# A two-layer decoder trunk on one core: rows of x loaded once under a pinned first half-step, and six output columns side by side in the memory attention

## The chip, the cores and the metric

The kernel runs on one core of a Trainium2 chip. A core has a matrix engine (TensorE, PE in the rows, with PEld for its weight loads), a vector engine (VectorE, DVE), a scalar engine (ScalarE, ACT), GpSimd (POOL) and a queue engine (SyncE, SP) that here issues most DMAs. Each takes its own instructions in the order of its program and waits on semaphores for the others. The metric is the device time of one execution in microseconds; lower is better.

## The reference

Two decoder layers act on x, 256 tokens of 1024 features, with a memory of 256 tokens. All weights are float32 and each is used once.

```
for l in range(DEPTH):
    x = x + 0.5 * swiglu(rmsnorm(x, ffn1_norm[l]), ffn1_w_gate[l], ffn1_w_up[l], ffn1_w_down[l])
    h = rmsnorm(x, mix_norm[l])
    x = x + (even_mixer(h, ...) if l % 2 == 0 else odd_mixer(h, ...))
    x = x + memory_cross_attention(rmsnorm(x, xa_norm[l]), mem_n, xa_w_q[l], xa_w_kv[l], xa_w_o[l])
    x = x + 0.5 * swiglu(rmsnorm(x, ffn2_norm[l]), ffn2_w_gate[l], ffn2_w_up[l], ffn2_w_down[l])
return rmsnorm(x, final_norm)
```

`swiglu` is `(silu(x @ w_gate) * (x @ w_up)) @ w_down` with 2816 hidden features. `memory_cross_attention` has 4 heads of 128 features: queries from x, keys and values from the memory, a softmax, and an output projection `o @ w_o` from 512 to 1024 features.

## The kernel before, in words

**Layout.** x stays in SBUF with features on the partitions, as 8 tiles of 128 features by 256 tokens (`x[:, k]`). Weights are a stream of 128x128 tiles in the order of their use: `Stream.take` returns the next. They come from HBM in chunks of 16 tiles (1 MB, four `raw` buffers); blocks of 8 tiles are split into a high part (`whi`, ACT, line 127) and a low part (`wlo`, DVE, line 128: raw minus high), with five buffers of each. A product is done as high by high and low, plus low by high. In the feed-forward step (`mm`, lines 391 and 392) that is one matmul of 512 columns with `whi` and one of 256 with `wlo`; elsewhere (`mm_narrow`, lines 396 to 398) it is three of 256 columns.

**The first half-step** (`ffn1` of layer 0). `w0` holds, for each of the 8 feature tiles, a row of x and four gate-weight tiles side by side (384 KB); `load_first` loads all eight, and later x itself is loaded once more from `xT` in one copy of 1 MB. `gates` runs four gate columns (f = 0 to 3) side by side as the rows land, in two `acc` and two `sc` banks of PSUM. After it `gate_up` does one column at a time: 16 matmuls on one `acc` bank, then `join` (ACT copies one half, DVE adds the other). The sum of squares of x (`squares`) and its mean (`norm_scale`: a small matmul in `sums`, a power on POOL, a transposing matmul in `spread`, an ACT copy into `rbc`) run beside the matmuls. Until `rbc` is there, finished columns wait in `n.waiting`; then `evac` multiplies the gate by `rbc` (DVE), takes the Silu (ACT), multiplies by the up column (DVE) and splits the result into `h` (high part ACT, low part DVE).

**What sets the order.** The builder, `Order`, keeps a clock of PE's work: fillers (the matmul groups) are written out in turn, and tasks put in with `pe.after(delay, fn, cost)` fall in between. That gives a program order, which the framework's scheduler then rearranges for each engine by its own estimates, save for instructions that are marked with `tc.keep_in_program_order`. In `memory` the weight splits are so marked (`ws.pin`).

**The memory attention.** Each of the 4 heads goes through scores, softmax, a turn (`go_turn`, transposing matmuls, line 708, then a split of the probabilities on ACT and DVE, lines 710 and 711) and a weighing with the values (`go_weigh`, lines 725 to 729), whose result is split into `h` (lines 459 and 460). `out_proj` multiplies these four `h` tiles by `w_o`. Columns 0 to 3 stand side by side in four `acc` banks and are fed in parts (heads 0 and 1, then head 2, then head 3); columns 4 to 7 follow one after the other with all four heads. A finished column is added to x (`add_to_x`, DVE, line 454), and the normed tile for the next half-step is made from it (ACT line 316, DVE line 317).

## Time and profile before

| | |
|---|---|
| three timed runs | 970.76, 971.33, 971.44 us; median 971.33 |
| profiled execution | 971.57 us, of which the span of the core's instructions is 969.8 |
| PE busy | 959.2 us, 99% of the span |
| DVE, ACT, POOL busy | 760.2, 614.1, 55.7 us |
| granted TensorE clock | 0.999 of full speed over the span |
| HBM read | 193.51 MB |

The profiled execution lies 0.24 us above the median of the timed ones. Busy time of a matmul in the profile includes the overlap with its neighbours, so PE's 99% is no statement that it runs at its peak; stretches in which fewer matmuls start tell more.

### The profile page before, as it was taken

How to read it: one execution, taken by the hardware profiler on the slowest of the kernel's cores; microseconds unless marked ns; L12 is line 12 of the kernel's file. 1: busy time of each engine (PE TensorE's matmuls, PEld its weight loads, DVE VectorE, ACT ScalarE, POOL GpSimd, SP SyncE). 2: the span in 40 equal slices, each digit the busy share in tenths (PEclk: the TensorE clock that was granted, in tenths of full speed). 3: DMA queues.
4: the chain of work that ended last, by engine and by line, in shares of the span. 5: the costliest groups of instructions: out<-in, count | busy, mean ns of one | idle time of the engine just before them, and what ended most of it. 6: DMA issues, size and time to landing. Idle time of an engine off the chain costs nothing.

```text
span 969.8 us, 16906 instructions
## 1 busy us (share of the span) xinstructions
PE 959.2 (99%) x6536; PEld 899.6 (93%) x6536; DVE 760.2 (78%) x1361; ACT 614.1 (63%) x1144; POOL 55.7 (6%) x95
## 2 busy tenths in 40 slices
PE   9999999999999999999999999999999999999997
PEld 8899999999999999999999999999999999999896
DVE  7988867898878888876778878677878789887663
ACT  7767655697657766665556666556785667666541
POOL 0410000001000000000000000000000003400011
PEclk9999999999999999999999999999999999999999
DMA  9797556555536656556555565565645346775631
GB/s 372 272 333 284 187 205 211 170 189 196 190 111 211 231 191 215 194 198 215 184 208 198 193 218 184 207 208 183 223 147 189 116 167 242 243 253 187 212 131 44
DMA packets 29921, 196.73 MB, mean 203 GB/s; under 512 B 3848, under 2 KB 4872, under 8 KB 7184
## 3 DMA queue, kind: packets, MB, share of 16 engines
q1 hardware_dynamic: 27072, 187.44, 55.5%
q0 software_dynamic: 2192, 7.37, 2.2%
q8 instruction: 51, 0.84, 0.3%
q10 hardware_dynamic: 576, 0.83, 0.2%
q14 instruction: 30, 0.25, 0.1%
HBM read 193.51 MB, written 5.27 MB: 205 GB/s over the span
## 4 chain that ended last, share of the span: by engine, by line
PE 97%; DVE 1%; DMA 1%; ACT 0%; issue 0%; SPq 0%; POOLq 0%; DVEq 0%; ACTq 0%
PE acc L391 41%; PE acc L392 21%; PE acc L397 7%; PE acc L398 7%; PE acc L396 7%; PE acc L574 1%; PE acc L573 1%; PE acc L572 1%; PE acc L918 1%; PE acc L916 1%; PE acc L917 1%; DMA raw<-in_w 1%; PE sc L572 0%; PE sc L574 0%; PE sc L573 0%; DVE wlo L128 0%
## 5 line engine op out<-in xcount | busy, mean ns | idle before, releaser
L127 ACT ACTIVATE whi<-raw 128x1024 fp32r<-128x1024 f32 (+2 forms) x377 | 369.2, 986 | 274.0 <-PE acc L391 133.3
L128 DVE TENSOR_TENSOR wlo<-raw,whi 128x1024 fp32r<-128x1024 f32 (+2 forms) x377 | 426.6, 1136 | 144.7 <-ACT whi L127 141.6
L391 PE MATMUL acc<-x,whi 128*128 128x512 f32 x1392 | 457.4, 383 | 0.9 <-DVE w L402 0.5
L392 PE MATMUL acc<-x,wlo 128*128 128x256 f32 x1392 | 377.4, 273 | 0.6 <-DVE wlo L128 0.6
L391 PEld LDWEIGHTS acc<-x,whi 128*128 128x128 f32 x1392 | 262.2, 189 | 37.4 <-ACT whi L127 1.1
L392 PEld LDWEIGHTS acc<-x,wlo 128*128 128x128 f32 x1392 | 267.2, 192 | 1.9 <-DVE wlo L128 0.9
L391 PE MATMUL acc<-h,whi 128*128 128x512 f32 x462 | 151.3, 382 | 0.0
L392 PE MATMUL acc<-h,wlo 128*128 128x256 f32 x462 | 125.4, 273 | 0.0
L391 PEld LDWEIGHTS acc<-h,whi 128*128 128x128 f32 x462 | 87.1, 189 | 12.0
L392 PEld LDWEIGHTS acc<-h,wlo 128*128 128x128 f32 x462 | 88.7, 192 | 0.2
L396 PE MATMUL acc<-h,whi 128*128 128x256 f32 x322 | 87.2, 279 | 1.6 <-ACT h L459 1.6
L397 PE MATMUL acc<-h,whi 128*128 128x256 f32 x322 | 88.1, 276 | 0.3 <-DVE h L460 0.3
L398 PE MATMUL acc<-h,wlo 128*128 128x256 f32 x322 | 87.8, 275 | 0.0
L402 DVE TENSOR_TENSOR w<-acc,w 128x256 f32<-128x256 f32 x195 | 81.1, 416 | 3.8 <-ACT w L401 3.5
L398 PE MATMUL acc<-x,wlo 128*128 128x256 f32 x304 | 83.9, 278 | 0.0
L397 PE MATMUL acc<-x,whi 128*128 128x256 f32 x304 | 83.8, 277 | 0.0
L396 PE MATMUL acc<-x,whi 128*128 128x256 f32 x304 | 83.4, 279 | 0.0
L401 ACT ACTIVATE w<-acc 128x256 f32<-128x256 f32 x195 | 71.9, 369 | 10.0 <-PE acc L392 9.8
L396 PEld LDWEIGHTS acc<-h,whi 128*128 128x128 f32 x322 | 60.5, 192 | 2.6 <-ACT h L459 2.0
L397 PEld LDWEIGHTS acc<-h,whi 128*128 128x128 f32 x322 | 61.7, 192 | 0.8 <-DVE h L460 0.7
L398 PEld LDWEIGHTS acc<-h,wlo 128*128 128x128 f32 x322 | 61.7, 192 | 0.1
L397 PEld LDWEIGHTS acc<-x,whi 128*128 128x128 f32 x304 | 58.2, 192 | 0.2
(211 smaller groups left out, 1180.7 us busy)
## 6 DMA issues: line engine op xcount, KB each, us to landing
raw<-in_w SPq DMA_DIRECT2D x171, 1024.0 KB, 5.0
dists<-line POOLq DMA_DIRECT2D x2, 1536.0 KB, 13.3
raw<-in_memT SPq DMA_DIRECT2D x3, 1024.0 KB, 5.1
raw<-in_w SPq DMA_DIRECT2D x6, 384.0 KB, 6.8
bias<-dists POOLq DMA_DIRECT2D x2, 1024.0 KB, 11.3
x<-in_xT SPq DMA_DIRECT2D x1, 1024.0 KB, 7.6
tok<-q POOLq DMA_DIRECT2D x32, 32.0 KB, 3.5
bias<-tok POOLq DMA_DIRECT2D x1, 1024.0 KB, 7.7
```

The lines of the kernel that those rows point to most:

```text
L127: for ins in (self.nc.scalar.activation(hi[:, at], src, AF.Copy), self.nc.vector.tensor_tensor(lo[:, at], src, hi[:, at].bitcast(F32), op= ...
L128: self.nc.vector.tensor_tensor(lo[:, at], src, hi[:, at].bitcast(F32), op=ALU.subtract)):
L391: nc.tensor.matmul(ps, w[0], x2.both, start=start, stop=False)
L392: nc.tensor.matmul(ps[:, :S], w[1], x2.high, start=False, stop=stop)
L396: nc.tensor.matmul(ps[:, :S], w[0], x2.high, start=start, stop=False)
L397: nc.tensor.matmul(ps[:, :S], w[0], x2.low, start=False, stop=False)
L398: nc.tensor.matmul(ps[:, :S], w[1], x2.high, start=False, stop=stop)
L401: nc.scalar.activation(halves(out), unpaired(ps[:, S:]), AF.Copy)
L402: nc.vector.tensor_tensor(halves(out), unpaired(ps[:, :S]), halves(out), op=ALU.add)
L572: nc.tensor.matmul(ps, hh, wh, start=f == 0, stop=False)
L573: nc.tensor.matmul(ps, hh, wl, start=False, stop=False)
L574: nc.tensor.matmul(ps, hl, wh, start=False, stop=f == FT - 1)
```

## The change

The first part is the start. `load_first` now brings feature tiles 2 to 7 of x straight into `x` by three copies of 256 KB (two tiles each), the gate weights of rows 2 to 7 by six of 256 KB without x beside them, and at the end tiles 0 and 1 of x by another; the later 1 MB copy is gone, and the POOL instruction ahead of it. From the end of `gates` until the first columns are evacuated, nearly all instructions of the half-step are kept in program order (`pe.kept`); blocks are split two ahead instead of four (`ws.ahead`); the squares go by four pairs; and the evacuation of the waiting columns is cut into steps (`evac_steps`: `gate`, `high`, `low`) that are placed 1300 ns of PE time apart, columns 2000 ns apart.

The second part is `out_proj` of the memory attention in both layers: six columns side by side instead of four, the fifth and sixth in the two `sc` banks, and then two instead of four.

```diff
@@ Stream
+        self.ahead = 2
-    def load_first(self):
+    def load_first(self, x, xT):
...
+            if k % 2 == 0 and k > 0:
+                self.nc.sync.dma_start(x[:, k:k + 2], xT[:, k:k + 2])
-            cuts = (0, S + P, STEP) if k == 0 else (0, STEP)
+            cuts = (0, S + P, STEP) if k == 0 else (0, STEP) if k == 1 else (S, STEP)
...
-            rows.append(t[:, o:o + S])
+            rows.append(t[:, o:o + S] if k < 2 else x[:, k])
+        self.nc.sync.dma_start(x[:, :2], xT[:, :2])
...
-        self._due_to(b + 1 + self.AHEAD_BLOCKS)
+        self._due_to(b + 1 + self.ahead)
@@ build
+    def keep(ins):
+        return tc.keep_in_program_order(ins) if pe.kept else ins
...
-            pe.after(*((2200, spread, 120) if wide else (1400, known, 0)))
+            pe.after(*((2900 if pe.kept else 2200, spread, 120) if wide else (1400, known, 0)))
@@ known
-            for fn in n.waiting:
-                fn()
+            n.pending = len(n.waiting)
+            for i, fn in enumerate(n.waiting):
+                pe.after(i * 2000, fn, 0) if pe.kept else fn()
@@ mm (and the same in squares, sums, spread and join)
-        nc.tensor.matmul(ps, w[0], x2.both, start=start, stop=False)
-        nc.tensor.matmul(ps[:, :S], w[1], x2.high, start=False, stop=stop)
+        keep(nc.tensor.matmul(ps, w[0], x2.both, start=start, stop=False))
+        keep(nc.tensor.matmul(ps[:, :S], w[1], x2.high, start=False, stop=stop))
@@ gates
+            pe.kept, ws.pin = True, tc.keep_in_program_order
+            ws.fill()
+            for k in range(4):
+                squares(n, k, x, KT)
+            ws.fill()
             for f in range(SIDE):
                 cur[f, 0] = join(w1(), cur[f, 0])
+            ws._due_to(FIRST // BLK + 3)
+            ws.fill()
+            for k in range(4, KT):
+                squares(n, k, x, KT)
@@ gate_up
                 if ks[-1] == KT - 1:
+                    if pe.kept:
+                        ws.flush()
                     cur[f, part] = join(w1(), ps)
@@ evac
+            if pe.kept:
+                evac_steps(f, g, u)
+                return
...
+        def evac_steps(f, g, u):
+            def gate():
+                keep(nc.vector.tensor_tensor(g, g, n.rbc, op=ALU.mult))
+                keep(nc.scalar.activation(g, g, AF.Silu))
+                pe.after(1300, high, 0)
+            def high():
+                keep(nc.vector.tensor_tensor(u, g, u, op=ALU.mult))
+                h[f] = h_tile()
+                keep(nc.scalar.activation(h[f].hi, halves(u), AF.Copy))
+                pe.after(1300, low, 0)
+            def low():
+                keep(nc.vector.tensor_tensor(h[f].lo, halves(u), h[f].hi.bitcast(F32), op=ALU.subtract))
+                n.pending -= 1
+                if not n.pending:
+                    pe.kept, ws.pin, ws.ahead = False, None, ws.AHEAD_BLOCKS
+            gate()
@@ ffn
-        if first:
-            for k in range(KT):
-                pe.after(12000 + 1800 * (k // 2), lambda k=k: squares(n, k, x), 0)
-        norm_scale(n, 18900 if first else 2300, unpin=True, turn=not first)
+        norm_scale(n, 16500 if first else 2300, unpin=True, turn=not first)
@@ out_proj
-    def out_proj(name, layer, o, nxt, early):
+    def out_proj(name, layer, o, nxt, early, side=4):
-        for js, cuts in ((range(0, 4), (0, *early, n_k)), (range(4, 8), (0, n_k))):
+        for js, cuts in ((range(0, side), (0, *early, n_k)), (range(side, KT), (0, n_k))):
...
-                        ps[j] = acc_tile()
+                        ps[j] = sc_tile() if 4 <= j < side else acc_tile()
@@ memory
-        pe.run(f[0] + f[1] + v[0] + f[2] + f[3] + v[1] + out_proj("xa_w_o", layer, o, nxt, (2, 3)))
+        pe.run(f[0] + f[1] + v[0] + f[2] + f[3] + v[1] + out_proj("xa_w_o", layer, o, nxt, (2, 3), side=6))
@@ end of build
-        if k == KT // 2 - 1:
-            nc.gpsimd.tensor_copy(x[:, 0, :1], block[1][:, :1].bitcast(F32))
-            nc.sync.dma_start(x, a["xT"])
```

Line numbers of the changed kernel are higher: split 132 and 133, matmuls 402 and 403, `mm_narrow` 407 to 409, join 412 and 413, add to x 465, normed tile 322 and 323, `h` split 470 and 471, weighing 770 to 774, steps of the evacuation 563 to 574. Every engine keeps nearly the same number of instructions, and the order differs in three places only: the first half-step, and the memory attention's end in each layer.

ACT in the first half-step, around the copy `rbc`. Before (the third line is `rbc`; `w1` under line 526 are the gates under Silu, 459 makes `h`):

```order
L127 ACTIVATE whi_405<-raw_325 128x1024
L127 ACTIVATE whi_464<-raw_325 128x1024
L367 ACTIVATE rbc_401<-tr_398 128x256
L127 ACTIVATE whi_545<-raw_388 128x1024
L526 ACTIVATE w1_236<-w1_236 128x256
L526 ACTIVATE w1_239<-w1_239 128x256
L526 ACTIVATE w1_242<-w1_242 128x256
L526 ACTIVATE w1_245<-w1_245 128x256
```

And now on the same engine (Silu is line 564, `h` line 570, the copy of `join` line 412):

```order
L377 ACTIVATE rbc_381<-tr_378 128x256
L564 ACTIVATE w1_251<-w1_251 128x256
L570 ACTIVATE h_397<-w1_294 128x2x128
L132 ACTIVATE whi_407<-raw_276 128x1024
L412 ACTIVATE w1_411<-acc_385 128x256
L564 ACTIVATE w1_254<-w1_254 128x256
L570 ACTIVATE h_427<-w1_318 128x2x128
L132 ACTIVATE whi_437<-raw_276 128x1024
```

Splits that stood ahead of the evacuation now stand between its steps; `whi_437` is the fourth block after `spread`, and `whi_476`, the fifth, follows seven instructions later.

PE in the memory attention, from the weighing of head 2 (`tr_3853`) on. Before, the weighing of head 3 (`tr_3889`) stands behind six matmuls with head 2's `h_3860`:

```order
L729 MATMUL tr_3853<-p2_3799,bias_3427 128x256
L396 MATMUL acc_3831<-h_3860,whi_3715 128x256
L396 MATMUL acc_3865<-h_3860,whi_3715 128x256
L396 MATMUL acc_3872<-h_3860,whi_3715 128x256
L396 MATMUL acc_3879<-h_3860,whi_3715 128x256
L397 MATMUL acc_3831<-h_3860,whi_3715 128x256
L398 MATMUL acc_3831<-h_3860,wlo_3716 128x256
L725 MATMUL tr_3889<-p2_3845,bias_3427 128x256
```

Now 12 more matmuls of heads 0 and 1 (into `sc_3885` and `sc_3906`) stand before this place, and the transposes of head 3 (line 753, two lines) are moved back by them; the two weighings follow each other:

```order
L753 MATMUL tr_3839<-ident_93,w2_3775 128x128 x2
L409 MATMUL acc_3878<-h_3695,wlo_3672 128x256
L770 MATMUL tr_3852<-p2_3798,bias_3426 128x256
L773 MATMUL tr_3852<-p2_3799,bias_3426 128x256
L774 MATMUL tr_3852<-p2_3798,bias_3426 128x256
L770 MATMUL tr_3892<-p2_3844,bias_3426 128x256
L773 MATMUL tr_3892<-p2_3845,bias_3426 128x256
L774 MATMUL tr_3892<-p2_3844,bias_3426 128x256
L407 MATMUL acc_3830<-h_3859,whi_3714 128x256
```

DVE behind it, where the columns are added to x and the next half-step's tiles are made. Before, from the fourth column's add to the second normed tile (`x_3929`):

```order
L454 TENSOR_TENSOR x_69<-acc_3879,x_69 128x256
L317 SCALAR_TENSOR_TENSOR x_3916<-x_69,vecs_70,x_3916 128x2x128
L128 TENSOR_TENSOR wlo_3900<-raw_3743,whi_3899 128x512
L454 TENSOR_TENSOR x_69<-acc_3951,x_69 128x256
L128 TENSOR_TENSOR wlo_3922<-raw_3743,whi_3921 128x1024
L317 SCALAR_TENSOR_TENSOR x_3929<-x_69,vecs_70,x_3929 128x2x128
```

Now, to the second normed tile (`x_3954`):

```order
L465 TENSOR_TENSOR x_69<-acc_3878,x_69 128x256
L465 TENSOR_TENSOR x_69<-sc_3885,x_69 128x256
L323 SCALAR_TENSOR_TENSOR x_3937<-x_69,vecs_70,x_3937 128x2x128
L465 TENSOR_TENSOR x_69<-sc_3906,x_69 128x256
L133 TENSOR_TENSOR wlo_3903<-raw_3742,whi_3902 128x512
L465 TENSOR_TENSOR x_69<-acc_3995,x_69 128x256
L133 TENSOR_TENSOR wlo_3943<-raw_3742,whi_3942 128x1024
L133 TENSOR_TENSOR wlo_3947<-raw_3831,whi_3946 128x1024
L465 TENSOR_TENSOR x_69<-acc_4019,x_69 128x256
L323 SCALAR_TENSOR_TENSOR x_3954<-x_69,vecs_70,x_3954 128x2x128
```

All eight adds and three weight splits now stand before the second normed tile.

## Rows read from the trace of the kernel before

**Rows 1.** The page: span, busy time of each engine, chain by engine.

```profile
span 969.8 us, 16906 instructions
PE 959.2 (99%) x6536; PEld 899.6 (93%) x6536; DVE 760.2 (78%) x1361; ACT 614.1 (63%) x1144; POOL 55.7 (6%) x95
...
PE 97%; DVE 1%; DMA 1%; ACT 0%; issue 0%; SPq 0%; POOLq 0%; DVEq 0%; ACTq 0%
```

**Rows 2.** PE's waits over the span: us in total, times, longest.

```profile
PE acc L396 <- ACT h L459: 1.6, 2, 0.8
...
PE acc L392 <- DVE wlo L128: 0.6, 1, 0.6
PE acc L391 <- DVE w L402: 0.5, 1, 0.5
PE acc L391 <- DVE x L317: 0.4, 1, 0.4
```

**Rows 3.** PE in four stretches: length, busy (matmuls), clock, DMA share, GB/s.

```profile
304.14:309.31 5.17, 4.21 (x34) 1.00 0.25 74
309.31:314.65 5.34, 5.34 (x48) 1.00 1.01 345
779.75:784.91 5.16, 4.20 (x34) 1.00 0.33 90
60.00:100.00 40.00, 40.00 (x246) 1.00 0.83 299
```

**Rows 4.** PE's timeline, first half-step: start, length, then the instruction.

```profile
16.36 0.76 PE L391 MATMUL acc<-x,whi 128*128 128x512 f32 x2
16.95 0.37 PE L392 MATMUL acc<-x,wlo 128*128 128x256 f32 x1
...
21.86 0.61 PE L391 MATMUL acc<-x,whi 128*128 128x512 f32 x2
23.07 0.38 PE L392 MATMUL acc<-x,wlo 128*128 128x256 f32 x1 [0.60 <-DVE wlo L128]
...
39.01 0.27 PE L392 MATMUL acc<-x,wlo 128*128 128x256 f32 x1
39.78 0.45 PE L391 MATMUL acc<-x,whi 128*128 128x512 f32 x1 [0.50 <-DVE w L402]
```

**Rows 5.** All engines in two stretches; the last number is the DMA rate in GB/s.

```profile
5.00:10.00 5.00, 4.57 (x25) 3.79 (x25) 3.79 (x8) 3.99 (x9) 0.37 (x1) 1.00 1.02 398
14.50:20.00 5.50, 5.50 (x35) 4.83 (x34) 4.29 (x7) 5.30 (x12) 0.00 (x0) 1.00 1.01 423
```

**Rows 6.** ACT's timeline, first half-step.

```profile
7.25 0.51 ACT L316 ACTIVATE x<-raw,vecs 128x256 fp32r<-128x256 f32 x1 [1.01 <-DMA raw<-in_w]
...
14.57 2.00 ACT L127 ACTIVATE whi<-raw 128x1024 fp32r<-128x1024 f32 x2 [1.45 <-DMA raw<-in_w]
...
34.93 1.32 ACT L526 ACTIVATE w<-w 128x256 f32<-128x256 f32 x4
```

**Rows 7.** DVE's timeline: first half-step, then behind the memory attention.

```profile
15.67 2.36 DVE L128 TENSOR_TENSOR wlo<-raw,whi 128x1024 fp32r<-128x1024 f32 x2 [1.68 <-ACT whi L127]
...
33.58 1.42 DVE L525 TENSOR_TENSOR w<-w,rbc 128x256 f32<-128x256 f32 x4
...
308.83 1.41 DVE L454 TENSOR_TENSOR x<-acc,x 128x256 f32<-128x256 f32 x4
310.16 0.47 DVE L317 SCALAR_TENSOR_TENSOR x<-x,vecs 128x256 fp32r<-128x256 f32 x1
310.55 0.68 DVE L128 TENSOR_TENSOR wlo<-raw,whi 128x512 fp32r<-128x512 f32 x1
```

**Rows 8.** The memory attention's end: PE's and ACT's timelines at head 3's turn.

```profile
302.47 0.38 PE L708 MATMUL tr<-ident,w 128*128 128x128 f32 x2
303.36 0.38 PE L708 MATMUL tr<-ident,w 128*128 128x128 f32 x2
...
303.78 0.60 ACT L710 ACTIVATE p<-tr 128x512 fp32r<-128x512 f32 x1 [0.82 <-PE tr L708]
```

**Rows 9.** SP's issues at the start, and a landing: issues, KB, us from issue to landing.

```profile
0.74 4.55 SPq L87 DMA_DIRECT2D raw<-in_w  x8
...
raw<-in_w SPq DMA_DIRECT2D x6, 384.0 KB, 6.8
```

More of the change, by code (lines that the diff above doesn't have):

```diff
@@ L184, in __init__ @@
         self.n = 0
+        self.kept = False
     def after(self, delay, fn, cost):
@@ L274, in build @@
     nc.scalar.dma_start(vecs, a["vecs"])
-    first_rows = ws.load_first()
+    first_rows = ws.load_first(x, a["xT"])
     ws._load_to(ws.n_loaded + 1)
@@ L319, in normed_tile, with squares @@
             squares(n, k, stream)
-    def squares(n, k, stream):
-        if k < KT - 2:
+    def keep(ins):
+        return tc.keep_in_program_order(ins) if pe.kept else ins
+    def squares(n, k, stream, pairs=KT - 2):
+        if k < pairs:
             if k % 2 == 0:
@@ L326, in squares @@
             sq = w2()
-            nc.scalar.activation(sq, stream[:, k - 1:k + 1].rearrange("p k s -> p (k s)"), AF.Square)
+            keep(nc.scalar.activation(sq, stream[:, k - 1:k + 1].rearrange("p k s -> p (k s)"), AF.Square))
             if k == 1:
@@ L330, in squares @@
             else:
-                nc.vector.tensor_tensor(n.acc, n.acc, sq, op=ALU.add)
-            if k == KT - 3:
+                keep(nc.vector.tensor_tensor(n.acc, n.acc, sq, op=ALU.add))
+            if k == pairs - 1:
                 two, n.acc = n.acc, act.tile([P, S], F32, name="sqacc", bufs=2)
-                nc.vector.tensor_tensor(n.acc, two[:, :S], two[:, S:], op=ALU.add)
+                keep(nc.vector.tensor_tensor(n.acc, two[:, :S], two[:, S:], op=ALU.add))
         else:
@@ L353, in sums @@
                 else:
-                    nc.tensor.matmul(pt[:, t:t + 1], part, ones, start=True, stop=True)
+                    keep(nc.tensor.matmul(pt[:, t:t + 1], part, ones, start=True, stop=True))
             if turn:
                 nc.vector.tensor_reduce(ms, halves(pt[:, :S]), axis=AX.X, op=ALU.add)
-            nc.vector.tensor_scalar(ms, ms if turn else pt[:, :2], 1.0 / D, EPS, op0=ALU.mult, op1=ALU.add)
+            keep(nc.vector.tensor_scalar(ms, ms if turn else pt[:, :2], 1.0 / D, EPS, op0=ALU.mult, op1=ALU.add))
             n.rcol = act.tile([P, 2], F32, name="rcolm" if n.keep else "rcol", bufs=1 if n.keep else 2)
             nc.gpsimd.tensor_tensor(n.rcol, ms, mhalf, op=ALU.pow)
-            pe.after(*((2200, spread, 120) if wide else (1400, known, 0)))
+            pe.after(*((2900 if pe.kept else 2200, spread, 120) if wide else (1400, known, 0)))
         def spread():
@@ L364, in spread @@
             for t in range(2):
-                nc.tensor.transpose(pt[:, t * P:(t + 1) * P], n.rcol[:, t:t + 1].to_broadcast([P, P]), ident)
+                keep(nc.tensor.transpose(pt[:, t * P:(t + 1) * P], n.rcol[:, t:t + 1].to_broadcast([P, P]), ident))
             n.rbc = act.tile([P, S], F32, name="rbcm" if n.keep else "rbc", bufs=1 if n.keep else 2)
-            nc.scalar.activation(n.rbc, pt[:, :S], AF.Copy)
+            keep(nc.scalar.activation(n.rbc, pt[:, :S], AF.Copy))
             known()
@@ L372, in known @@
             ws.fine = False
-            if unpin:
+            if unpin and not pe.kept:
                 ws.pin = None
-            for fn in n.waiting:
-                fn()
+            n.pending = len(n.waiting)
+            for i, fn in enumerate(n.waiting):
+                pe.after(i * 2000, fn, 0) if pe.kept else fn()
             n.waiting = []
@@ L400, in join @@
     def join(out, ps):
-        nc.scalar.activation(halves(out), unpaired(ps[:, S:]), AF.Copy)
-        nc.vector.tensor_tensor(halves(out), unpaired(ps[:, :S]), halves(out), op=ALU.add)
+        keep(nc.scalar.activation(halves(out), unpaired(ps[:, S:]), AF.Copy))
+        keep(nc.vector.tensor_tensor(halves(out), unpaired(ps[:, :S]), halves(out), op=ALU.add))
         return out
@@ L514, in go @@
                 if ks[-1] == KT - 1:
+                    if pe.kept:
+                        ws.flush()
                     cur[f, part] = join(w1(), ps)
                     if part == 1:
+                        if n.ready and pe.kept:
+                            n.pending += 1
                         when_scaled(n, lambda: evac(f, cur[f, 0], cur[f, 1]))
```

## The prediction

> **What bounds the kernel now.** I read the page first: PE is busy 959.2 of 969.8 us and the chain that ended last is 97% PE [rows 1]. The change removes no matmul, so only time in which PE stands still can be won or lost. PE's waits [rows 2] add up to little and name two kinds of place. Twice it waits 0.8 us for `h` of the memory attention; three times, 0.4 to 0.6 us, for DVE in the first half-step. I then sized these places by starts, since busy time hides part of a stall.
>
> In the memory attention 34 matmuls of 256 columns stand in 5.17 us, and right behind it 48 in 5.34 us, 0.111 each [rows 3]. By the counts 5.17 - 34 x 0.111 = 1.4 us are lost; three of the 34 began before the stretch, which makes it 1.7. Layer 1 shows the same 34 in 5.16. In the feed-forward steps 246 matmuls take 40.00 us [rows 3], so a pair takes 0.326 (0.22 for the 512 columns, 0.107 for the 256) and a block of 8 pairs 2.6.
>
> In the first half-step the three stalls are read from starts [rows 4]: 16.36 to 16.95 holds two matmuls of 512 (0.43), so 0.16 is lost; 21.86 to 23.07 holds two as well, 0.78; 39.01 to 39.78 holds one of 256, 0.66. That is 1.6 us, with about 0.1 at each restart, 1.9.
>
> **The start, step by step.** *Loads.* Rows 2 to 7 come as the same bytes in another cut, and tiles 0 and 1 of x (262 kB) now stand ahead of the first weight chunk. At 398 GB/s [rows 5] that is 0.66 us. ACT got that chunk at 14.57 after 1.45 us of waiting [rows 6]; now at 15.23. The splits that follow are 1.04 on ACT (two take 2.00, so the next starts 0.96 after) [rows 6] and 1.21 on DVE (two take 2.36) [rows 7], with about 0.04 for each hand-over. PE reaches the block at 16.36 with its `whi` just there, issues 0.22, and its `wlo` is ready at 15.23 + 1.04 + 0.04 + 1.21 + 0.05 = 17.57: **1.0 us stall** (0.4 if the chunk lands as before). Row 2, for which ACT waits until 7.25 [rows 6], is about even: its x lands by bytes 0.3 earlier, its weights 0.3 later, and ACT makes two x tiles ahead of the split, so PE starts near 8.4 as now.
>
> *Behind it* PE runs blocks at 2.6: the second ends at 22.6, the two sums matmuls fall at 23.9 (the last add of the squares is done about 23.8 on DVE), the fourth ends at 28.2, where `spread` stands. The Square and add instructions and the POOL copy that fall away are hidden now, by PE's blocks; no gain. The 1 MB copy that goes brings later chunks about 2 us sooner, and in the walk none of them ends a wait.
>
> *The evacuation chain.* From `spread` I follow ACT and DVE in their new order. Small operations take 0.41 on either; the next starts 0.30 after on ACT (four in 1.32) [rows 6], 0.335 on DVE (four in 1.42) [rows 7]. PE's transpose reaches ACT 0.42 after it starts (303.36 to 303.78) [rows 8]. `rbc` runs 28.69 to 29.06 (behind the last join's copy), gate multiply on DVE to 29.57, Silu to 30.01, up multiply to 30.46, `h` high to 30.90, split of `whi_407` to 31.86, its low part to 33.11, join and next gate multiply to 33.78, Silu to 34.22, multiply to 34.67, `h` high to 35.11, split of `whi_437` to 36.07, its low part to 37.32. PE has had 0.2 + 3 x 2.62 + 0.22 of work since 28.2 and wants that low part at 36.5: **0.87 us stall**. Queued behind it on DVE are seven small operations (7 x 0.335, to 39.66), on ACT two `h` parts until 40.0, then `whi_476` to 41.05, a join copy, `whi_540` to 42.28; DVE's low part of 476 is there at 42.30. PE, restarted at 37.37, runs out at 40.21, as its next three matmuls want `whi_476`, `whi_540`, `wlo_476`: it goes on at 42.5, a **2.3 us stall**. After that the splits stay a block ahead of PE (the next low part at 45.0, wanted at 45.4).
>
> The sum of the start: 1.0 + 0.87 + 2.3 + 0.3 for three restarts = 4.5 lost, against 1.9 now: **+2.6 us**. The bounds: 0 lost if the hand-overs overlap more than the rows show (-1.9), 6 if each of the 13 steps of the chain takes 0.1 more (+4).
>
> **The memory attention, step by step** (layer 0; the order of layer 1 differs by the same instructions). The 12 added matmuls (1.33 us) push the second pair of head 3's transposes from 303.36 [rows 8] to 304.57. ACT's part of the turn is then 304.99 to 305.59 (0.60) [rows 8], DVE's ends 306.31. PE weighs head 2 until 305.57 and goes straight on to head 3, whose second matmul wants DVE's part: it starts at 306.35, not 305.74. That is **0.67 us of stall in place of 1.7**; behind it head 2's `h` is long there.
>
> Then the next half-step's entry. The first of the six columns is complete at 309.95 (six matmuls of head 2, 12 more, six and two of head 3 at 0.111). Before, the adds started at 308.83, and four columns still to be multiplied (48 matmuls, 5.34 us) [rows 3, 7] covered what DVE had to do. Now two columns cover it: PE is through them at 313.56. Until the second normed tile DVE has in its order eight adds at 0.335 (2.7), one normed tile (0.47, next after 0.40) [rows 7], a half split (0.60) and two whole ones (1.15 each) [rows 7], and that tile: 310.0 + 5.9 + 0.5 = 316.4. PE has its first tile by 312.2, so it starts, waits 0.3 for the low part of 3943, 1.0 for that of 3947 and 0.6 for the tile: **1.9 us stall** where there is none now. From there three columns share each tile (0.98 us of PE a tile against 0.40 to 1.0 on DVE) and PE isn't held again. Net: 0.67 + 1.94 - 1.7 = +0.9 a layer, **+1.8 us** for two. Bounds: -1.7 a layer if DVE keeps up, +1.5 if each of its ten instructions starts 0.06 later.
>
> **Sum.** 971.57 is the profiled execution's own time (span 969.8 and 1.8 around it). 971.57 + 2.6 + 1.8 = 975.97; that execution lies 0.24 above the median of 971.33, so I forecast **975.7 us**.
>
> **A rule weighed against the rows.** Six copies of 384 KB at the start take a median 6.8 us each from issue to landing [rows 9], while the core takes in 398 GB/s, which is 393 kB in 0.99 us [rows 5]: they overlap almost wholly, so cutting finer costs bytes, not latencies. The Trainium skill, page "DMA: Bandwidth & Descriptors", section "Measured (HBM→SBUF, 128 partitions, SWDGE, issued from GpSimd)", says "Batch DMAs to ≥1 MiB for ≥75% of peak", and the page's section "Anatomy of one DMA — SWDGE (gpsimd) path" puts a fixed 2.0 us on each. If the four additional copies each paid that in turn, the first chunk would be 8 us late and the time near 983, an estimate from that page; the overlap in the rows speaks against it, and I give it 0.02. A milder form, from rows, is a rival below.
>
> **Rivals.**
> *DVE isn't late* (faster). One mechanism at three places: low parts of splits are there when PE wants them. Its price is what I charge to DVE, 0.87 and 2.3 in the start and 1.9 in each layer, 7.0 in all: 975.7 - 7.0 = 968.7. The point at which it decides: `wlo_437` within 8.3 us of `spread` and the second normed tile within 4.4 us of the first complete column. For it: DVE was busy only 78% [rows 1], and before it did an add, a tile and a half split in 2.1 us after the adds without holding PE [rows 7]. Against: DVE and ACT take instructions in order, and the new order puts the late splits behind work that waits for the other engine.
> *Only one of the two parts is late* (no change). If the memory's cover holds (0.67 - 1.7 a layer, -2.1) and the start loses 2.6, 972; if the start is even and the memory loses 1.8, 973.1.
> *The loads are bound by issue* (slower still). SP spent 4.55 us on its first eight issues [rows 9], 0.57 each. Four additional ones would make the first chunk 2.3 us late, not 0.66: +1.6, 977.3. Against: data already ran at 398 GB/s then [rows 5]. For: smaller copies leave less in flight. The full latency of a copy, 6.8 us [rows 9], for one of the four would already make it worse than that.
> *The order does nothing*: the changed order is visible in the program, so this can only be a wash of the above.
>
> **How the numbers follow.** A difference under 0.2% (1.9 us) can hardly be told from no change here. Forecast 0.50 (973.5 to 976.9), loads bound by issue 0.10 (976.9 to 979), each copy's latency paid in turn 0.02 (above 979), one part late 0.18 (970 to 973.5), DVE not late 0.20 (967.5 to 969.5, with a little up to 970). The likeliest alone would be 973.5 to 976.9. The range leaves out half of the faster case and half of the case bound by issue, some 2 in 10: 968.7 to 977.5. Slower by over 0.2% (above 973.3): 0.62; within 0.2%: 0.19; faster (below 969.4): 0.19.
>
> **What would show it.** In the changed profile: PE waits for `wlo` near 16.6 us by about 1.0, near 36.5 by 0.9, near 40 by 2.3; ACT's wait for the first chunk ends near 15.2; in both layers PE waits 0.6 for DVE's part of the probabilities, and 1 to 2 us for `wlo` and a normed tile at the entry of the next half-step. If the waits at 304 and 780 are gone with nothing at 314 and 790, the memory step is wrong; if PE meets no `wlo` wait between 28 and 43, the evacuation chain is. The whole is wrong if the time is below 971.

## The result, and the profile after

The changed kernel takes 979.46 us (median of six runs, 978.17 to 980.75) against 971.38 (six runs, 970.76 to 971.79): a ratio of 1.0082, with an interval of 1.0071 to 1.0093. It is slower, as forecast, but by 8.1 us instead of 4.4, outside the range. The profiled execution took 979.68.

The page of the changed kernel has the same work in a longer span [rows 1]:

```profile
span 977.9 us, 16906 instructions
PE 962.6 (98%) x6536; PEld 900.9 (92%) x6536; DVE 760.7 (78%) x1360; ACT 614.2 (63%) x1143; POOL 52.5 (5%) x94
...
PE 94%; DVE 2%; DMA 1%; ACT 1%; issue 1%; SPq 0%; POOLq 0%; DVEq 0%; ACTq 0%
```

PE's waits over the span answer to [rows 2]: those for `h` are gone, and those for splits (`wlo`, `whi`) add up to 5.7 us instead of 0.6.

```profile
PE acc L403 <- DVE wlo L133: 3.1, 4, 0.9
PE acc L402 <- ACT whi L132: 2.6, 4, 1.3
PE tr L770 <- DVE p L756: 1.3, 2, 0.6
...
PE acc L402 <- DVE x L323: 0.7, 2, 0.4
```

Where they lie is seen in PE's timeline: the first half-step [rows 4], then the end of layer 0's memory attention.

```profile
8.96 0.70 PE L402 MATMUL acc<-x,whi 128*128 128x512 f32 x2 [0.42 <-ACT whi L132]
...
17.24 0.48 PE L402 MATMUL acc<-x,whi 128*128 128x512 f32 x1 [0.16 <-ACT whi L132]
18.50 0.38 PE L403 MATMUL acc<-x,wlo 128*128 128x256 f32 x1 [0.78 <-DVE wlo L133]
...
37.47 0.48 PE L402 MATMUL acc<-x,whi 128*128 128x512 f32 x1
38.80 0.38 PE L403 MATMUL acc<-x,wlo 128*128 128x256 f32 x1 [0.86 <-DVE wlo L133]
...
42.75 0.48 PE L402 MATMUL acc<-x,whi 128*128 128x512 f32 x1 [1.28 <-ACT whi L132]
43.97 0.79 PE L402 MATMUL acc<-x,whi 128*128 128x512 f32 x1 [0.73 <-ACT whi L132]
...
44.77 0.63 PE L402 MATMUL acc<-x,whi 128*128 128x512 f32 x1
...
47.33 0.38 PE L402 MATMUL acc<-x,whi 128*128 128x512 f32 x1
...
312.00 0.38 PE L770 MATMUL tr<-p,bias 128*128 128x256 f32 x1 [0.63 <-DVE p L756]
...
321.61 0.38 PE L403 MATMUL acc<-x,wlo 128*128 128x256 f32 x1 [0.76 <-DVE wlo L133]
322.34 0.48 PE L402 MATMUL acc<-x,whi 128*128 128x512 f32 x1 [0.35 <-DVE x L323]
```

Every late start but the first is where the prediction put it. Two things are not in its sum. From 43.97 to 47.33 stand five pairs of matmuls in 3.36 us, which take 5 x 0.326 = 1.63 elsewhere. And the first wait, at 8.96, is that for row 2, whose first matmul started at 8.42 before. ACT's timeline shows what came late by DMA: x tiles 2 and 3 at 7.30 (row 2 stood there at 7.25; ACT split its weights from 7.66 then, and from 8.28 now, behind two tiles of x), and the first weight chunk at 16.13, against 14.57 [rows 6].

```profile
7.30 0.91 ACT L322 ACTIVATE x<-x,vecs 128x256 fp32r<-128x256 f32 x2 [0.79 <-DMA x<-in_xT]
8.28 1.31 ACT L132 ACTIVATE whi<-raw 128x512 fp32r<-128x512 f32 x2
...
16.13 1.06 ACT L132 ACTIVATE whi<-raw 128x1024 fp32r<-128x1024 f32 x1 [2.51 <-DMA raw<-in_w]
```

The windows of three stretches show what lies behind both (the last three numbers are granted clock, DMA share and GB/s). Changed kernel:

```profile
4.50:7.00 2.50, 2.49 (x10) 1.76 (x10) 1.44 (x4) 1.44 (x3) 0.00 (x0) 1.00 0.95 260
41.00:44.00 3.00, 0.99 (x6) 0.40 (x4) 1.57 (x3) 3.00 (x7) 0.00 (x0) 0.98 0.69 284
44.00:48.00 4.00, 4.00 (x15) 3.48 (x16) 4.00 (x8) 3.33 (x5) 2.31 (x6) 0.59 0.68 209
```

And the first of them in the kernel before:

```profile
4.50:7.00 2.50, 2.49 (x13) 1.90 (x13) 1.74 (x4) 1.44 (x3) 0.00 (x0) 1.00 1.00 372
```

Loads ran at 260 GB/s instead of 372 while the DMA engines were nearly as busy (0.95 and 1.00); and the granted clock fell behind 3 us in which PE worked for 1.0.

To size the terms I followed the start of the same matmul (the first, second, ... of the span) in both traces. How late the changed kernel is, and what the prediction had:

| up to | late by, us | this step | predicted |
|---|---|---|---|
| row 2's first matmul (8.42, now 8.96) | 0.54 | +0.54 | 0 |
| first weight block (18.36, now 20.03) | 1.66 | +1.12 | +0.84 |
| the stall near 22 of before is gone (29.29, now 30.11) | 0.82 | -0.84 | -0.78 |
| fourth block after `spread` (36.83, now 39.02) | 2.19 | +1.37 | +0.87 |
| fifth and sixth (40.07, now 43.97), less the 0.66 of before | 3.90 | +1.71 | +1.64 |
| half clock over (41.71, now 47.33) | 5.62 | +1.72 | - |
| memory attention, layer 0 (323.50, now 330.19) | 6.69 | +1.07 | +0.9 |
| layer 1 (792.34, now 800.11) | 7.77 | +1.08 | +0.9 |

This sets one execution against one. The profiles of side5 and side6 (below), which have the old start, run that part 0.35 and 0.63 us earlier than the profile of the kernel before does, so the steps that hang on loads are known to about that.

### The profile page after: what moved, and what is told of

It is laid out like the page before. It is cut to its first block, busy times and chain, and to the rows that moved or that the text cites. A ratio compares the mean times of both kernels' runs of the same rounds, so it can differ in the third digit from the quotient of the medians.

```text
span 977.9 us, 16906 instructions
## 1 busy us (share of the span) xinstructions
PE 962.6 (98%) x6536; PEld 900.9 (92%) x6536; DVE 760.7 (78%) x1360; ACT 614.2 (63%) x1143; POOL 52.5 (5%) x94
## 4 chain that ended last, share of the span: by engine, by line
PE 94%; DVE 2%; DMA 1%; ACT 1%; issue 1%; SPq 0%; POOLq 0%; DVEq 0%; ACTq 0%
PE acc L402 40%; PE acc L403 20%; PE acc L407 7%; PE acc L409 7%; PE acc L408 7%; PE acc L621 1%; PE acc L622 1%; PE acc L620 1%; DMA raw<-in_w 1%; PE acc L962 1%; PE acc L961 1%; PE acc L963 1%; DVE wlo L133 1%; DVE x L465 1%; PE sc L620 0%
## 5 line engine op out<-in xcount | busy, mean ns | idle before, releaser
L403 PEld LDWEIGHTS acc<-x,wlo 128*128 128x128 f32 x1392 | 268.0, 193 | 5.7 <-DVE wlo L133 5.1
L403 PE MATMUL acc<-h,wlo 128*128 128x256 f32 x462 | 125.5, 273 | 0.0
L402 PEld LDWEIGHTS acc<-h,whi 128*128 128x128 f32 x462 | 87.1, 189 | 12.0
L403 PEld LDWEIGHTS acc<-h,wlo 128*128 128x128 f32 x462 | 88.7, 192 | 0.2
L409 PE MATMUL acc<-h,wlo 128*128 128x256 f32 x306 | 83.7, 276 | 0.0
L408 PE MATMUL acc<-h,whi 128*128 128x256 f32 x306 | 83.3, 275 | 0.0
L407 PE MATMUL acc<-h,whi 128*128 128x256 f32 x306 | 82.1, 277 | 0.0
L408 PEld LDWEIGHTS acc<-h,whi 128*128 128x128 f32 x306 | 58.7, 192 | 0.1
L409 PEld LDWEIGHTS acc<-h,wlo 128*128 128x128 f32 x306 | 58.7, 192 | 0.1
L409 PEld LDWEIGHTS acc<-x,wlo 128*128 128x128 f32 x304 | 58.2, 192 | 0.1
```

The source lines that it names most:

```text
L402: keep(nc.tensor.matmul(ps, w[0], x2.both, start=start, stop=False))
L403: keep(nc.tensor.matmul(ps[:, :S], w[1], x2.high, start=False, stop=stop))
L407: nc.tensor.matmul(ps[:, :S], w[0], x2.high, start=start, stop=False)
L408: nc.tensor.matmul(ps[:, :S], w[0], x2.low, start=False, stop=False)
L409: nc.tensor.matmul(ps[:, :S], w[1], x2.high, start=False, stop=stop)
```

## The experiments

All ratios are to runs of the kernel before on the same chip (medians of 971.55 to 971.71 us).

**The two parts apart.** Each is a part of the diff shown above: the kernel before with `side=6`, the changed kernel with `side=4`, and the kernel before with `side=5`.

> The kernel before with six columns side by side in the memory attention's output projection and nothing else changed. If what the memory step lost in the changed kernel (1.07 and 1.08 us of later matmuls in layers 0 and 1) comes from the six columns alone, this is 2.1 us over the kernel before, with PE waits of 0.8 for the probabilities' low part at the weighing and about 0.2, 1.0 and 0.6 us at the entry of the next half-step, in both layers. Rival: that loss is in part an echo of the new first half-step (another rotation of the weight buffers); then it is 0 to 1 us over.

Measured: 973.69, ratio 1.0021 (1.0012 to 1.0030): 2.1 us, as expected. By matched starts it loses 1.07 and 1.08 in the two layers, with the same waits: the rival of an echo is out.

> The changed kernel with four columns side by side again in the memory attention: the whole of the new start and nothing else. If the parts add, it is 5.6 to 6.0 us over the kernel before where the granted clock falls near 44 us, and some 4.2 to 4.6 where it does not, with the waits near 17, 37, 41 and 43 us as in the changed kernel. If the prediction's sum for the start were right after all and the rest were an interplay, it would be 2.6 over.

Measured: 976.57 (975.52 to 978.56), ratio 1.0052 (1.0039 to 1.0064): 5.0 us, so the parts add up to 7.1 of the 8.1. One of its five runs had a mean granted clock of 0.995 (978.56); of the changed kernel's six, four had 0.997 (979.24 to 980.75) and two 0.999 (978.17, 978.87), which is about the rest. (Its four runs at 0.998 and 0.999 lie 4.0 to 5.1 us over the kernel before, where 4.2 to 4.6 was expected.) The 2.6 of the prediction is ruled out.

> The kernel before with five columns side by side in the memory attention's output projection, three after them. If the loss of six is a matter of cover (two columns of 1.33 us behind the first complete ones, for about 6 us of DVE's work), three columns take away some 1.3 us of the 1.9 us at the next half-step's entry, while about half of the 1.7 us at the weighing is still saved: 0.4 us a layer faster to 0.2 slower, 970.6 to 971.8 in all. If each column more costs the same, it is 1.05 us over the kernel before.

Measured: 970.53, ratio 0.9989 (0.9981 to 0.9998): faster than both kernels, and just below the expected 970.6 to 971.8. PE's waits in it:

```profile
PE tr L725 <- DVE p L711: 1.5, 2, 0.7
...
PE acc L392 <- DVE wlo L128: 0.6, 1, 0.6
PE acc L391 <- DVE w L402: 0.5, 1, 0.5
```

The wait for the probabilities stands at the weighing as with six columns, the waits at the next half-step's entry are gone. Each column behind the first complete ones is 1.33 us of cover, and with three of them DVE is in time: the loss is one of cover, not of columns as such.

**The loads.**

```diff
@@ loads: the kernel before with the new load_first, and without its later copy
-            nc.gpsimd.tensor_copy(x[:, 0, :1], block[1][:, :1].bitcast(F32))
-            nc.sync.dma_start(x, a["xT"])
@@ pairs: the changed kernel, weights of two rows in one copy, packets of 2 KB
+                self.nc.sync.dma_start(t[:, :2 * STEP].rearrange("p (k s) -> p k s", k=2)[:, :, S:],
+                                       self.first[k:k + 2].rearrange("k p s -> p k s")[:, :, S:])
@@ big: the same with packets of 4 KB
+                self.nc.sync.dma_start(t[:, :BLK * P], wp[k // 2 - 1])
@@ dense: the changed kernel, its copies out of blocks that are unbroken in memory
-                self.nc.sync.dma_start(x[:, k:k + 2], xT[:, k:k + 2])
+                self.nc.sync.dma_start(x[:, k:k + 2], xp[k // 2])
...
+                (self.nc.scalar if k == 1 else self.nc.sync).dma_start(t[:, o + i:o + j], self.first[k][:, i:j] if k < 2 else wp[k - 2])
@@ rows23: the changed kernel
-            cuts = (0, S + P, STEP) if k == 0 else (0, STEP) if k == 1 else (S, STEP)
+            cuts = (0, S + P, STEP) if k == 0 else (0, STEP) if k < 4 else (S, STEP)
...
+        self.nc.sync.dma_start(x[:, :4], xT[:, :4])
@@ x01_late: the changed kernel
-        self.nc.sync.dma_start(x[:, :2], xT[:, :2])
...
     ws._load_to(ws.n_loaded + 1)
+    nc.sync.dma_start(x[:, :2], a["xT"][:, :2])
```

> The kernel before with only the new loading of x and of the first weights (three copies of x tiles ahead of their weights, tiles 0 and 1 last, no later copy of 1 MB); order and evacuation of the half-step as the scheduler makes them. If the finer cut itself delays the first weight chunk, ACT's wait for that chunk ends near 16.1 us (14.6 before) and the time is 1.0 to 1.7 us over the kernel before. If only the 262 kB ahead of it count, it ends near 15.2 and the time is 0.3 to 0.6 over. If the pinned order were what cost at this place, the time would be that of before.

> The changed kernel with the first weights of rows 2 to 7 brought by three copies of 512 KB instead of six of 256 KB: the same bytes in the same packets of 2 KB, with three issues less. If SP's issues and their waits for earlier landings delay the first weight chunk, ACT's wait for it ends at 15.2 to 15.6 us instead of 16.1, and the time is 0.5 to 0.9 us below the changed kernel. If the packets are slow themselves, the rate from 4.5 to 7 us stays at 170 to 260 GB/s, the gates' matmuls end at 15.6 or later, and the time is that of the changed kernel.

> As the kernel with three copies of 512 KB, but these weights lie together in memory, so that their packets are 4 KB instead of 2 KB; the copies of x keep 2 KB. If the size of the packets limits the rate at the start, it is above 300 GB/s from 5 to 7 us, row 2 is there a little earlier and the time is 0.7 to 1.4 us below that of the kernel with three copies and packets of 2 KB. If the cause lies in the number or the order of copies, both take the same time.

> The changed kernel with x's pairs of tiles and the weights of rows 2 to 7 each lying in memory as one unbroken block of 256 KB; number, order, size and packets (2 KB) of the copies stay. Before, each packet was 2 KB out of 8 (x) or of 3 KB (weights). If reading with such gaps makes the start slow, the rate from 4.5 to 7 us is over 330 GB/s, x tiles 2 and 3 are there by 7 us, the gates' matmuls end near 15.0 (six profiles of the gapped kind: 15.6 to 16.6) and the time is about 1.3 us below the changed kernel. If the size of the packets or the number of copies does it, rate (223 to 298 in those profiles) and time stay.

> The changed kernel with rows 2 and 3 loaded as in the kernel before (x and four weight tiles together, 384 KB in packets of 3 KB), and x tiles 0 to 3 by one copy of 512 KB at the end. If the slow stretch comes from cutting rows 2 and 3 into x and weights early in the program, the rate from 4.5 to 7 us is 370 GB/s as before the change and the gates' matmuls end by 15.0; 262 kB more ahead of the first chunk delay it by 0.66, so that of 1.4 us about 0.8 are left as gain over the changed kernel. If not, the gates end at 15.6 or later.

> The changed kernel with the copy of x tiles 0 and 1 issued behind the first weight chunk instead of ahead of it. By bytes the chunk lands 0.66 us earlier; in the changed kernel ACT gets it 0.3 to 0.6 us after the gates' last matmul, so then about 0.2 before, and PE's 1.05 us stall for the first low part shrinks to about 0.4: 0.6 us below the changed kernel. If the issue of the chunk is held by earlier landings and not by bytes, it lands as late as now less one issue (0.3 us), and the gain is 0.2 to 0.3.

Where these expectations speak of the end of the gates' matmuls, their times belong to a matmul eight records ahead of the first one behind the gates; the table gives the latter. It is read from each trace as the lines above; `x` is when ACT had x tiles 2 and 3 (row 2 in the kernel before).

| kernel | GB/s, 4.5 to 7 | x | first chunk at ACT | first matmul behind the gates | time, ratio |
|---|---|---|---|---|---|
| before | 372 | 7.25 | 14.57 | 16.36 | |
| changed | 260 | 7.30 | 16.13 | 17.24 | 979.46, 1.0082 (1.0071 to 1.0093) |
| start4 | 234 | 8.30 | 16.73 | 17.84 | as above |
| loads | 223 | 8.47 | 17.20 | 18.31 | 973.04, 1.0013 (1.0004 to 1.0022) |
| pairs | 247 | 7.54 | 16.02 | 17.48 | 978.35, 1.0067 (1.0054 to 1.0079) |
| big | 298 | 7.85 | 16.41 | 17.75 | 977.83, 1.0063 (1.0050 to 1.0077) |
| dense | 347 | 6.88 | 15.37 | 16.48 | 977.29, 1.0067 (1.0054 to 1.0081) |
| rows23 | 361 | - | 16.39 | 17.50 | 979.36, 1.0081 (1.0067 to 1.0094) |
| x01_late | 233 | 8.44 | 16.39 | 17.89 | 980.42, 1.0089 (1.0075 to 1.0102) |

The loads alone cost 1.5 us, with the order of the kernel before: they are a cause of their own. The copies as the change cuts them run at 208 to 260 GB/s in all eight profiles that have them, and row 2's first matmul comes 0.5 us late in the changed kernel's own profile, the mildest, and up to 1.7 in others. In loads the first chunk came even later (17.20) than expected (16.1). Fewer copies of the same packets (pairs) leave the rate where it was, so the number of issues is not what bounds it: SP issues the first chunk at 7.09 there, as early as in the kernel before (6.99; 9.01 in the changed kernel), and ACT still gets it at 16.02.

```profile
7.09 8.08 SPq L109 DMA_DIRECT2D raw<-in_w  x4
```

In big the weights have larger packets and lie without gaps, two things at once; the rate is 298 (312 from 5 to 7 us, where over 300 was expected), but x comes no earlier, and the time is 0.5 us below that of pairs with intervals that overlap. Unbroken blocks for x and weights, with number, order and packets of the copies unchanged (dense), bring 347 and x by 6.88:

```profile
4.50:7.00 2.50, 2.31 (x12) 1.83 (x12) 1.63 (x4) 1.56 (x4) 0.00 (x0) 1.00 1.02 347
```

joined and joined2 (below) have these blocks too: 346, and 315 in joined2, where already the second part of row 0 came later (ACT had it at 5.24 us, in dense at 4.84). The packets tell the same. Those of 2 KB that start from 4.5 to 7 us take on average 93 to 96 ns in these three traces and 108 to 138 ns in the eight with gaps; from 7 to 9 us they take 84 to 90 in all eleven. The chip is not the reason: x01_late and rows23 ran on the same one as dense.

So it is the reading out of rows with gaps, 2 KB of each 8 KB for x and of each 3 KB for weights, that made the start slow. The blocks of dense are other tensors, at other addresses; that this matters is not ruled out by dense alone, but rows23 reads whole rows of the old tensor at 361 GB/s. The Trainium skill, page "DMA: Bandwidth & Descriptors", section "Latency and other measured facts", reports slower copies at row pitches of 2 MiB and more than at 512 KiB, and advises to pad the pitch or to lay tiles out contiguously. Its figures don't cover pitches of 3 and 8 KB; the runs here agree with the second advice. By time, dense stands 2.2 us under the changed kernel, with intervals that overlap; against that one's two runs without a fall of the clock (978.17 and 978.87) it is 1.2, about the 1.3 expected. Its rate and its first matmul (16.48) are the evidence, more than its median.

rows23 shows the same from the other side: rows 2 and 3 in time, 361 GB/s, and the slow stretch moved to where the first gapped copy of x now stands (284 GB/s from 7 to 9 us; 397 there in the changed kernel):

```profile
7.00:9.00 2.00, 2.00 (x14) 1.81 (x13) 2.00 (x4) 1.40 (x4) 0.00 (x0) 1.00 1.01 284
```

The expected gain of 0.8 us did not come (979.36 against 979.46): the chunk, with 262 kB more ahead of it, reached ACT at 16.39, and PE waits 1.18 us for its high part. x01_late missed its expectation too: it is 1.0 us above the changed kernel, not 0.2 to 0.6 below, with intervals that overlap. Its chunk reached ACT at 16.39, against 16.73 and 17.20 in start4 and loads, whose rows were as late; but the squares of tiles 0 and 1, pinned ahead of the second split on ACT, now wait for the copy.

```profile
16.39 1.06 ACT L131 ACTIVATE whi<-raw 128x1024 fp32r<-128x1024 f32 x1 [2.03 <-DMA raw<-in_w]
18.01 1.15 ACT L337 ACTIVATE w<-x 128x512 f32<-128x512 f32 x2 [0.56 <-DMA x<-in_xT]
19.07 1.04 ACT L131 ACTIVATE whi<-raw 128x1024 fp32r<-128x1024 f32 x1
```

**The evacuation.**

```diff
-        self.ahead = 2
+        self.ahead = 4
```

> The changed kernel with its weight splits made four blocks ahead instead of two while the half-step is kept in program order; every split then stands one block (2.6 us of PE) earlier in ACT's and DVE's order. If the stalls near 37, 41 and 43 us (1.1, 1.4 and 1.0 us) come from splits that stand behind the steps of the evacuation, a block earlier leaves at most 1 us of them, the granted clock doesn't fall after them, and the time is 4 us below the changed kernel: 975 to 976. If the evacuation's chain is too long wherever the splits stand, the stalls only move: 979 to 980.

Measured: 976.65 (975.62 to 976.99), ratio 1.0049 (1.0035 to 1.0063), 2.8 us below the changed kernel. (Its order shows two more splits ahead of `rbc` on ACT, so the lead is two blocks more, not one as the expectation says.) In its profile PE doesn't wait once between 32 and 60 us; what is left of the waits for splits lies at the first chunk and in the memory attention. The 2.8 us hold the stalls and the fall of the clock behind them, which none of its four runs has (0.998 and 0.999). It is 0.65 us over the expected upper end; its trace shows two losses that can account for that: rows came 1 us later than in the changed kernel's profile (the 1.8 in the first line), and a new wait of 1.1 us stands at the norm's `spread`. There the small DVE instruction that makes the mean of squares now has three splits queued ahead of it behind the last add of the squares, in the changed kernel one.

```profile
PE acc L402 <- DVE x L323: 2.5, 3, 1.8
PE acc L403 <- DVE wlo L133: 2.3, 3, 0.8
PE tr L770 <- DVE p L756: 1.3, 2, 0.6
PE tr L375 <- POOL rcol L369: 1.1, 1, 1.1
...
PE acc L402 <- ACT whi L132: 0.2, 1, 0.2
```

**The clock.** Nine matmuls whose result nothing reads are put where PE stands still for `whi_476`; in late_fill the same on top of x01_late, whose clock fell most often.

```diff
+                if first and len(ws.order) == 12 * BLK:
+                    pt = tr_tile()
+                    for i in range(9):
+                        tc.keep_in_program_order(nc.tensor.matmul(pt, ws.split[11][0][:, :P], n.x[0].both, start=True, stop=True))
```

> The changed kernel with nine matmuls of 512 columns more (their result is not used), placed in PE's order where it stands still for the split near 41.3 us; they take 1.9 us and end before the second late split is there at 43.97, so the stall ends when it did. If the fall of the granted clock to half speed at 44 to 47 us comes from PE's standstill, it stays at full speed and the time is 1.4 to 1.7 us below the changed kernel in runs in which that one's clock falls: about 978.0 in all runs. If the clock falls for another reason, the time stays at 979.5.

Measured: 979.33 (978.22 to 980.03). Inconclusive: the clock stayed at 1.00 in the profile, but the scheduler's order behind the nine had changed, and a new wait of 0.97 us for a `join` stands at 69 us. One of five runs had a mean clock of 0.996.

> The kernel with tiles 0 and 1 of x copied behind the first chunk, and in it the nine matmuls of 512 columns whose result is not used, in PE's order where it stands still near 42 us. That kernel's mean granted clock was 0.995 to 0.997 in three of its four runs, with half speed from 44 to 48 us. If PE's standstill brings the clock down, nearly all runs now are at 0.998 or more, and the median is 1.4 us or more below that of the same kernel without the nine, if no new wait arises behind them. If not, runs at 0.997 and less stay as frequent.

> The same kernel without the nine matmuls, once more, for comparison on one chip: by the first four runs, half or more of its runs at a mean clock of 0.997 or less, those 1.4 us and more above the others, median near 980.

Measured: 978.82 (978.55 to 978.94) with the nine, all five runs at a mean clock of 0.998 or 0.999; 979.20 (977.78 to 981.04) without, one of five at 0.997, and three of four the time before. Both expectations on time failed: the medians differ by 0.4 us, not by 1.4 or more, because four of the five runs without the nine show no fall this time (0.998 or 0.999). The windows with the nine, then without:

```profile
41.00:44.00 3.00, 3.00 (x18) 2.67 (x16) 1.56 (x5) 2.75 (x7) 0.01 (x1) 1.00 0.80 320
44.00:48.00 4.00, 3.66 (x22) 3.02 (x21) 4.00 (x8) 4.00 (x7) 2.07 (x6) 1.00 0.28 72
```

```profile
41.00:44.00 3.00, 1.64 (x11) 1.26 (x9) 1.57 (x5) 2.54 (x7) 0.74 (x2) 1.00 0.89 341
44.00:48.00 4.00, 3.27 (x11) 2.58 (x12) 4.00 (x8) 4.00 (x6) 2.31 (x6) 0.69 0.49 152
```

Over all runs of which the clock is listed: with this standstill, 12 of 39 had a mean of 0.997 or less; with the standstill filled, 1 of 10; without it (the kernel before and six others), 1 of 125. The fall belongs to the standstill, then, but doesn't always follow it. The counts are rough, since the mean over the span also holds its end: in all 17 profiles the clock is at half again for the last 1.3 to 4.4 us, after PE's last matmul (in the kernel before that matmul ended at 963.7 and the clock was at half from 967.4 on).

```profile
964.00:967.40 3.40, 0.00 (x0) 0.00 (x0) 1.85 (x6) 0.61 (x1) 0.70 (x1) 1.00 0.14 47
967.50:969.80 2.30, 0.00 (x0) 0.00 (x0) 0.00 (x0) 0.00 (x0) 0.00 (x0) 0.50 0.41 143
```

So a PE without any work does lose its clock here. That PE's idle time is also what brings it down at 44 us, where it still had some work, is likely by this and by the counts and not settled by them: 1 of 10 against 12 of 39 could be chance.

**The mends together.** joined is dense with `ahead = 4` and `side=5`. joined2 also copies x tiles 0 and 1 behind the first chunk and squares them last, and splits blocks three ahead until `spread`, four from there on (`off` is 2 in `gates`):

```diff
-        self.nc.sync.dma_start(x[:, :2], xp[0])
     ws._load_to(ws.n_loaded + 1)
+    nc.sync.dma_start(x[:, :2], a["xp"][0])
...
-            keep(nc.scalar.activation(sq, stream[:, k - 1:k + 1].rearrange("p k s -> p (k s)"), AF.Square))
+            keep(nc.scalar.activation(sq, stream[:, (k - 1 + off) % KT:(k - 1 + off) % KT + 2].rearrange("p k s -> p (k s)"), AF.Square))
...
         def spread():
+            if pe.kept:
+                ws.ahead = 4
```

> The kernel with the unbroken blocks, splits four blocks ahead, and five columns side by side in the memory attention: each of the three mends of the changed kernel. If they add (1.3 for the blocks, 2.8 measured for the splits, 2.1 + 1.0 measured for five columns instead of six), 979.5 - 7.2 = 972.3; the rest over the kernel before with five columns (970.5) is the wait for the first chunk and 1.1 us at the spreading of the norm. If the blocks give nothing, 973.6.

> The kernel with three mends (unbroken blocks, splits further ahead, five columns; 971.8) with the two waits mended that its trace still has: x tiles 0 and 1 are copied behind the first chunk and squared last, so that the chunk lands 0.66 us earlier and the 0.75 us wait for its low part falls to 0.1 to 0.2; and the splits run three blocks ahead until the norm is spread and four from there on, so that the mean of squares is not queued behind two splits and the 1.1 us wait at the spread falls to 0.2 or less. If these two are what is left of the loss against the kernel before with five columns (970.5), the time is 970.0 to 970.4. If the splits late in the evacuation come back, it stays at 971 to 972.

Measured: joined 971.77, ratio 1.0002 (0.9993 to 1.0011), 7.7 us below the changed kernel where the sum of the mends was 7.2; joined2 969.72, ratio 0.9980 (0.9971 to 0.9988), the fastest here; both lie a little below what was expected (972.3, and 970.0 to 970.4). All of PE's waits that the view lists for joined2 (the second lies ahead of the first row, the third within row 0):

```profile
PE tr L772 <- DVE p L758: 1.5, 2, 0.7
PE tr L295 <- DVE warm L277: 1.1, 1, 1.1
PE acc L404 <- ACT whi L131: 0.6, 1, 0.6
PE acc L405 <- DVE wlo L132: 0.5, 1, 0.5
```

The wait at `spread` and those of the evacuation are gone; that for the first low part fell from 0.75 to 0.52 only. Against five columns alone (970.53, on another chip) the intervals of the ratios overlap: the mended start is not shown to be better than the old one.

## Why the prediction was right or wrong

**Right:** the direction, and the place and cause of every stall that it named. PE waited for `wlo` of the first chunk, for the fourth block after `spread` (0.87 forecast, 0.86 in the profile, 1.1 by starts), for `whi` of the fifth and the sixth (2.3 forecast, where its list of signs says `wlo`; 2.4 by starts), and at all four places of the memory attention (0.67 forecast, 0.8 by starts; 1.9 forecast, 1.9 by starts). ahead4, side6 and side5 show that the stated causes are the causes: splits queued behind work that waits for the other engine, and too little cover for DVE. The rival that DVE isn't late is ruled out.

**Wrong: the load step.** "Row 2 ... is about even: its x lands by bytes 0.3 earlier, its weights 0.3 later" and the 0.66 us for the chunk took the 398 GB/s of [rows 5] for the new copies. Those are read with gaps and ran at 260 in this profile, at 208 in another. Row 2 was 0.5 us late instead of even and the chunk 1.56 instead of 0.66; the loads alone measured 1.5 us. That "cutting finer costs bytes, not latencies" was right as to latencies (dense has as many copies and is in time), but the layout in memory was not considered at all. The rival of loads bound by issue had the size of the delay (2.3 us for the chunk; 1.6 to 2.6 measured) with another cause; pairs speaks against its mechanism. The time fell above 979, where the prediction had put only 0.02, on each copy's latency paid in turn; that mechanism, with the chunk 8 us late, did not occur.

**Wrong: a term is missing.** The sum has no price for what PE's clock does behind a long standstill. The forecast stall of 2.3 us was followed by 3.4 us at half speed in four of the eight profiles that have it, which cost 1.7 us in the profiled execution and, by the two groups of its runs (0.997 and 0.999), about 1.3 in the timed ones that have it. What sets off the fall in one execution and not in the next stays open.

**Sizes off:** the memory attention 1.07 instead of 0.9 a layer, most of it the weighing's 0.8 for 0.67 (the prediction's own times, 306.35 for 305.74, give 0.61), since the wait stands before head 3's first matmul and not before its second; the evacuation 3.08 instead of 2.51, of which about 0.4 are longer waits and 0.2 the restarts that the sum had apart. With the loads (0.82), the clock (1.72) and the memory (0.35) that makes 3.46; less 0.06 for the stall near 22 it is the 3.4 that the table's last column lacks.

## What to carry to other kernels

When a load is cut anew, ask how its rows lie in memory, not only for bytes, packets and number of copies: the same copies out of unbroken blocks were on time. When an order is pinned, every split or copy that PE needs next has to stand ahead of chains that go back and forth between two engines; two blocks more of lead were worth 2.8 us here, the clock included. When columns are put side by side, count what is left behind the first complete one as cover for the engine that empties them: three columns were enough and a gain, two were not and a loss.

## What the runs showed of the hardware

Copies of 2 KB pieces out of rows of 8 KB (x) and 3 KB (weights) were slow only where the first of them stood (208 to 260 GB/s from 4.5 to 7 us in eight profiles; in rows23, 284 from 7 to 9); later ones of the same kind ran at 368 to 397 from 7 to 9 us in those eight. Why the first suffer stays open. And TensorE's granted clock fell from full speed (2.4 GHz) to half (1.2 GHz) behind 3 us in which PE had still worked for 1.0 us (changed kernel); it did so in four of the eight profiles that have this standstill (start4, pairs, big and dense stayed at 1.00), at the same place in the program each time.
